# Half of the mixer's convolution and attention output products by seven block products on tiles of 2x2 blocks

## The chip, the cores and the metric

The kernel runs on one core of one Trainium2 chip. The metric is the device time of one execution in microseconds, the median of several runs. A core has five engines with a queue each: TensorE (PE in the profile; its weight loads are listed apart as PEld), VectorE (DVE), ScalarE (ACT), GpSimd (POOL) and SyncE (SP), which here issues the transfers of the weights. An engine takes the instructions of its queue in order, and a semaphore holds an instruction back until what it needs is there.

## The reference, cut to what matters

Two layers of a streaming encoder step work on 640 tokens (512 of a new stream, 8 x 16 of running streams), 1024 wide, in float32. Each layer is a feed-forward half step, a mixer, and a second feed-forward half step. The change is in the mixer, whose last part is:

```
g = jax.nn.sigmoid(g + b_gate)
g_conv, g_attn = jnp.split(g, 2, axis=-1)
y_conv, conv_new = _short_conv(cb, cc, cv, conv_prev, w_conv)      # 512 channels
k_new, v_new, y_attn = ...                                         # attention, 8 heads x 64 = 512 channels
m = g_conv * (y_conv @ w_conv_out) + g_attn * (y_attn @ w_attn_out)
return m @ w_o, conv_new, k_new, v_new
```

`y_conv @ w_conv_out` and `y_attn @ w_attn_out` are products of 640x512 with 512x1024. All the outputs of the step (both token groups, the new keys, values and convolution states) are written.

## The kernel before, in words

**Numbers.** Everything lies transposed: 128 channels on the partitions, the 640 tokens along the free axis. One output tile is 128 channels x 640 tokens. Every operand of a product is split into a high part (a cast to fp32r by ScalarE, which TensorE takes) and a low part (operand minus high part, by VectorE); a product is three matmuls, high x high, high x low and low x high (`multiply`, line 412; the first factor is the weight here, so the order is: weight high with both parts of the operand, then weight low). A matmul takes 320 tokens, half of a tile.

**Weights.** All weights come as one stream of slabs of 128x1024 (eight tiles of 128x128), in the order in which TensorE uses them; the host lays them out in `_stream` by the same list that the device code walks (`mixer_order`, line 114; `stages`, line 136, turns it into kinds of slabs). SyncE loads them into three buffers in turn. A *plain* slab is eight tiles of weights, read one by one by `product`. A *mixed* unit is two slabs in memory, of which VectorE forms sums, so that four slabs of weights come out: for seven block products instead of eight on 2x2 blocks (blocks over two output tiles, two halves of the contraction, two halves of the tokens). `source` (line 293) forms the raw slab, with these sums for a mixed unit:

```
elif arg == 1:
    flush()
    st = sums[n] = spool[0].tile([P, CH // 2], F32, tag="s6", name=f"s6_{n}", bufs=1)
    add(ra[:, h1], ra[:, h1], rb[:, h1])
    add(st, ra[:, h1], rb[:, h2])
    add(rb[:, h1], rb[:, h1], rb[:, h2])
```

and one more sum for the third slab of the unit. `prep` (line 332) casts a slab on ScalarE and notes its low part as pending; `flush` (line 348) issues the pending low parts on VectorE. `slab` (line 355) hands out the next slab and prepares the one two after it; with `hold` set, the low part waits for the next `flush` in the text. `quiet` hands out a slab without preparing one, `ahead` forms the sums of the next slab that isn't prepared.

**The mixer's second part**, `outputs` (line 1463), is what the change rewrites. Before it, attention and the first of the eight pairs of gate tiles have run. It issues its work in an order written out by hand, and TensorE, VectorE and ScalarE keep it (`ORDERED`). Its pieces:
- `gate_pair(m)` (line 1473): two tiles of the gates as seven block products of 12 matmuls, on three banks of PSUM `pa`, `pb`, `pc` (rows `qa`, `qb`, `qc`) out of four that go round. `qa` takes blocks one, three, five and seven: block one is copied out by ScalarE (`c1`, row `capsm`) before block three is added onto it, and so on. VectorE forms `u` and `g` from the blocks, multiplies by the norm's factor `rr`, ScalarE applies the sigmoid (line 1328). Between, VectorE does the low parts (`wlo`, line 350) of the next slabs, and `ahead` stands after block five. A function `then` can be hung in before block six.
- `out(m, y)` (line 1516): one tile of `y @ w` in one of two accumulators `py` that alternate, 4 tiles of contraction x 3 x 2 = 24 matmuls, and the product with the gate on VectorE (line 1524, for the convolution into `mm`; line 1526 for the attention, with a sum onto `mm` after it). A function `then` is called between the matmuls and that product.
- `take` splits the four tiles of `y` into high and low parts (line 235), `give` those of the finished `m`.

The order is: gate pair 2 with `take` of the convolution, outputs 0 to 3, then six times a gate pair (4, 6, 8, 10, 12, 14) with two outputs behind it: 4 to 7 of the convolution and, after a `take` of the attention in pair 8, 8 to 15, which are the attention's outputs 0 to 7. So each pair stands between outputs. After them comes `m @ w_o`, eight products of 48 matmuls (row `po`).

Of the kernel before, what the change touches and what calls it, by code (L numbers as in the profile page):

```python
# [10 lines left out]
F32 = mybir.dt.float32  # L11
# [5 lines left out]
P = 128  # L17
# [38 lines left out]
)  # L56

ROWS = (1, 2)

MARGIN = 2, 4  # L60
LEAN = {"a0": (1, 6), "b0": (1, 5), "a1": (1, 5), "b1": (1, 5)}
# [66 lines left out]


def kinds():  # L130
# [5 lines left out]
def stages():  # L136

    out, done = [], []

    def end(kind):  # L140
        done.append((kind, out[:]))
        out.clear()

    def plain(n):
        out.extend([8] * (n // 8) + [n % 8] * (n % 8 > 0))

    def ffn(name):
        held = 0
        for what, a in ffn_order(name):
            if what == "gu":  # L150
                plain(held)
                held = 0
                out.append("gu")
            elif what == "std":
                held += 2 * KT
            elif what == "cut":
                plain(held)
                held = 0
            elif what == "rows":
                plain(held)  # L160
                held = 0
                out.append("gu")
            elif what == "ends":
                held += KT * len(a)
            else:
                held += sum(len(js) for _, js in a)
        plain(held)

    for l in range(L):
        ffn(f"a{l}")  # L170
        end("ffn")
        held = 0
        for what, _ in mixer_order():
            if what == "mix":
# [12 lines left out]
def two(ps):  # L187
    return ps[:, :, :HT]


def halves(t):
    return t.rearrange("p (a b) -> p a b", a=2)
# [3 lines left out]
def trunk(ctx: ExitStack, tc: tile.TileContext, xin, wst, small, pbias, samplebias, kcache, vcache, gfin,  # L196
# [1114 lines left out]
    def mixer(l, after):  # L1311
        with tc.tile_pool(name=f"yp{l}", bufs=1, reuse_waits="tile") as yp, \
# [84 lines left out]
            with tc.tile_pool(name=f"gp{l}", bufs=1, reuse_waits="tile") as gp, \  # L1397
                 tc.manual_schedule(engines=ORDERED):
                hold[0] = True
                mo = outputs(l, gp, ops.X, st, cs, ycs, yas, sigmoid, gates)  # L1400
        ex = after()
        with tc.manual_schedule(engines=ORDERED):
            hold[0] = True
# [56 lines left out]
        def t5(self, kp):  # L1460
            self.parts(*(z[:, HT:] for z in self.h[2 * kp]), self.a[kp][:, 1])

    def outputs(l, gp, X, st, cs, ycs, yas, sigmoid, gates):


        rr, t1, t2 = st.rr, slice(0, HT), slice(HT, T)
        spare = [gp.tile([P, 2, T], F32, name=f"mm{l}_{i}") for i in range(2)]
        mm = ycs + [spare[i // 2][:, i % 2] for i in range(CT)]
        X11, X21, X22, XN6, XT5, XT7, XT4 = (X[i] for i in ("11", "21", "22", "N6", "T5", "T7", "T4"))
        c1, u2, c5 = cs  # L1470
        every = range(NP)
# [56 lines left out]
            flush()  # L1528

        yc, ya, mo = [], [], []  # L1530

        def take(y, name, srcs):
# [496 lines left out]
def _stream(i):  # L2029
# [9 lines left out]
    for l in range(L):  # L2039
        def ffn(name, gu, down):  # L2040
            g, u = _cols(gu[:, :FF]), _cols(gu[:, FF:])
            d = _cols(down)
            parts, held = [], []
            for what, a in ffn_order(name):
                if what == "gu":
                    if held:
                        parts.append(chunks(held))
                    held = []

                    parts.append(chunks([z[a][o::2] for z in (u, g) for o in range(2)]))  # L2050
# [24 lines left out]
        held = []  # L2075
        for what, m in mixer_order():
            if what == "v":
                out.append(v.reshape(KT // 2, 2, P, AW).transpose(0, 2, 1, 3).reshape(-1, P, CH))
            elif what == "mix":
                out.append(chunks(held))  # L2080
                held = []

                out.append(chunks([rows[name][a][o::2] for name, a in m for o in range(2)]))
            else:
# [73 lines left out]
```

## Time and profile before

| | |
|---|---|
| time, median of 3 runs | 2491.59 us (2491.12 to 2491.73) |
| profiled execution, its own time | 2491.9 us |
| its span | 2490.1 us |
| second part of the mixer, layer 0 | 636 to 778.6 us, 142.6 us |
| granted TensorE clock | 1.00 |

The page gives busy time by engine. A busy TensorE there is the union of overlapping matmuls, so the spacing of their starts is read for the price of one. In a list in order of time, a row is start, duration, engine, line, operation, output and inputs by the program's names, and in brackets the idle time ahead of it with what ended it. In the list by stretches each engine has its busy time in the stretch, with the number of instructions, then the granted clock, the share of the DMA engines and GB/s. Layer 1 repeats the second part from 1918 us on with the same spacings.

### The profile page before, as it was taken

To read this page: it belongs to the slowest core of one execution; us is meant where nothing else is said; L and a number is where in the kernel's file an instruction comes from. 1 tells how busy PE (TensorE), PEld (TensorE's weight loads), DVE (VectorE), ACT (ScalarE), POOL (GpSimd) and SP (SyncE) were. 2 spreads that over 40 slices of the span, in tenths; PEclk is the share of its full clock that TensorE was granted. 3 is DMA by queue.
4 is the path that set the end of the run, shared out by engine and by line. 5 is a ranking of instruction groups with operands and counts; after the bars stand their busy time and mean duration, and the time that the engine had idled before them with its cause. 6 is when DMAs were issued, how large, how long until landed. Compare 5 with 4: busy or idle time off the path is not lost.

```text
span 2490.1 us, 43907 instructions
## 1 busy us (share of the span) xinstructions
PE 2475.0 (99%) x17312; PEld 2422.6 (97%) x17312; DVE 2140.2 (86%) x3532; ACT 1355.9 (54%) x2151; POOL 294.9 (12%) x449
## 2 busy tenths in 40 slices
PE   9999999999999999999999999999999999999998
PEld 8999999889999999999999999998999999999998
DVE  7999998888777899998799999998886769999997
ACT  6555556665444555555665555556644455555555
POOL 0111112211000001111001111121110000111111
PEclk9999999999999999999999999999999999999999
DMA  4443444335223333444334343453342233444444
GB/s 155 126 117 101 123 119 121 114 107 174 77 83 112 94 101 106 112 117 121 98 94 109 110 119 101 115 128 111 128 157 86 77 110 91 108 112 107 111 117 117
DMA packets 109422, 279.22 MB, mean 112 GB/s; under 512 B 12416, under 2 KB 51456, under 8 KB 109216
## 3 DMA queue, kind: packets, MB, share of 16 engines
q1 hardware_dynamic: 68976, 219.44, 26.9%
q0 software_dynamic: 39520, 56.08, 12.0%
q8 instruction: 135, 2.21, 0.4%
q10 hardware_dynamic: 720, 0.91, 0.1%
q14 instruction: 71, 0.58, 0.1%
HBM read 230.56 MB, written 7.94 MB: 96 GB/s over the span
## 4 chain that ended last, share of the span: by engine, by line
PE 93%; DVE 4%; ACT 2%; issue 1%; DMA 0%; ACTq 0%; SPq 0%; DVEq 0%; POOLq 0%
PE pab L440 12%; PE paa L440 11%; PE pcb L440 6%; PE daa L1118 6%; PE pca L440 5%; PE dab L1118 5%; PE py L416 4%; PE po L416 4%; PE qa L440 4%; PE pbb L440 3%; PE dca L1118 3%; PE pba L440 3%; PE dcb L1118 2%; PE ma_cv L440 2%; PE ma_qk L440 2%; PE pv L1605 2%
## 5 line engine op out<-in xcount | busy, mean ns | idle before, releaser
L350 DVE TENSOR_TENSOR wlo<-raw,whi 128x1024 fp32r<-128x1024 f32 (+1 forms) x569 | 580.3, 1022 | 156.1 <-ACT whi L345 152.9
L345 ACT CAST whi<-raw 128x1024 fp32r<-128x1024 f32 (+1 forms) x569 | 505.1, 891 | 381.7 <-PE pbb L440 47.2
L345 ACT CAST whi<-s 128x1024 fp32r<-128x1024 f32 (+1 forms) x158 | 150.3, 952 | 296.0 <-issue 111.3
L440 PE MATMUL pab<-xhib,whi 128*128 128x320 f32 x704 | 217.7, 309 | 0.0
L440 PE MATMUL pab<-xlob,whi 128*128 128x320 f32 x704 | 217.3, 309 | 0.0
L440 PE MATMUL pab<-xhib,wlo 128*128 128x320 f32 x704 | 217.3, 309 | 0.0
L440 PE MATMUL paa<-xloa,whi 128*128 128x320 f32 x640 | 197.6, 309 | 0.6 <-DVE xloa L677 0.6
L440 PE MATMUL paa<-xhia,whi 128*128 128x320 f32 x640 | 198.0, 309 | 0.2 <-DVE ga L287 0.2
L440 PE MATMUL paa<-xhia,wlo 128*128 128x320 f32 x640 | 197.6, 309 | 0.0
L350 DVE TENSOR_TENSOR wlo<-s,whi 128x1024 fp32r<-128x1024 f32 (+1 forms) x158 | 173.5, 1098 | 4.4 <-ACT whi L345 4.4
L1140 POOL DMA_DIRECT2D x<-c_a x80 | 69.9, 1021 | 574.9 <-ACT ahia L1022 205.6
L440 PEld LDWEIGHTS pab<-xhib,whi 128*128 128x128 f32 x704 | 132.1, 188 | 0.9 <-issue 0.9
L440 PEld LDWEIGHTS pab<-xhib,wlo 128*128 128x128 f32 x704 | 132.2, 188 | 0.0
L440 PEld LDWEIGHTS pab<-xlob,whi 128*128 128x128 f32 x704 | 132.2, 188 | 0.0
L1140 POOL DMA_DIRECT2D x<-c_b x72 | 62.7, 1001 | 582.9 <-ACT ahib L1022 205.8
L440 PEld LDWEIGHTS paa<-xhia,whi 128*128 128x128 f32 x640 | 120.1, 188 | 1.3 <-DVE ga L287 0.5
L440 PEld LDWEIGHTS paa<-xloa,whi 128*128 128x128 f32 x640 | 120.1, 188 | 1.1 <-DVE xloa L677 1.1
L440 PEld LDWEIGHTS paa<-xhia,wlo 128*128 128x128 f32 x640 | 120.1, 188 | 0.2
L440 PE MATMUL pcb<-xhib,wlo 128*128 128x320 f32 x352 | 108.9, 309 | 0.0
L440 PE MATMUL pcb<-xhib,whi 128*128 128x320 f32 x352 | 108.7, 309 | 0.0
L440 PE MATMUL pcb<-xlob,whi 128*128 128x320 f32 x352 | 108.7, 309 | 0.0
L287 DVE TENSOR_TENSOR raw<-s,raw 128x512 f32<-128x512 f32 x158 | 107.9, 683 | 0.0
(757 smaller groups left out, 8076.8 us busy)
## 6 DMA issues: line engine op xcount, KB each, us to landing
raw<-in_wst SPq DMA_DIRECT2D x375, 512.0 KB, 3.4
x<-c_a POOLq DMA_DIRECT2D x80, 160.0 KB, 4.4
x<-c_b POOLq DMA_DIRECT2D x72, 160.0 KB, 3.7
lent<-in_wst POOLq DMA_DIRECT2D x34, 256.0 KB, 3.7
kc<-in_kcache SPq DMA_DIRECT2D x32, 256.0 KB, 4.5
vc<-in_vcache SPq DMA_DIRECT2D x16, 512.0 KB, 4.5
x<-u_a POOLq DMA_DIRECT2D x40, 160.0 KB, 3.9
x<-u_b POOLq DMA_DIRECT2D x36, 160.0 KB, 4.0
```

The costliest lines, as they stand in the source:

```text
L287: DVE.tensor_tensor(out=out, in0=a, in1=b, op=op)
L345: ACT.copy(hi[:, d], src[:, c])
L350: DVE.tensor_tensor(out=lo, in0=src, in1=hi.bitcast(F32), op=ALU.subtract)
L416: PE.matmul(ps[:, a, :HT], w, x[a] if isinstance(x, tuple) else x[:, a * HT : (a + 1) * HT], start=first and j == 0 and not seeded, stop=l ...
L440: PE.matmul(ps, a, b, start=start and kp == 0 and j == 0, stop=stop and kp == NP - 1 and j == 2, skip_group_check=True)
L1118: PE.matmul(ps[u], w, y, start=start and i == 0 and j == 0, stop=i == 1 and j == 2, skip_group_check=True)
L1140: POOL.dma_start(x[ms[2 * u + r]][:, cols], z[:, u], accum_op=ALU.add)
L1605: PE.matmul(pv[t], xx[:, t * P : (t + 1) * P], w[:, kk * AW : (kk + 1) * AW], start=c == 0 and kk == 0 and j == 0, stop=c == KT // 2 - 1 a ...
```

## The change

In each branch four of the eight output tiles, 4 to 7 of the convolution and 2 to 5 of the attention (`SEVEN`), are computed together by a new function `rows`: four output tiles as 2x2 blocks, seven block products of 12 matmuls instead of four products of 24. Their weights come as mixed units, in the form of the gate pairs'. The operands of the seven products that are mixtures of tiles of `y` are made by a new function `mixed`, in the memory of `y` itself once its plain parts are taken, with a copy to high parts on ScalarE and a low part on VectorE; it is hung into outputs 0, 1 (and 2) of the branch, the last low part of the attention into gate pair 10. Outputs 0 to 3 now go into the spare tiles, 4 to 7 into the memory of the convolution's `y`. The order becomes: pair 2, outputs 0 to 3, pairs 4 and 6, `rows` for the convolution, pair 8, outputs 8 and 9, pairs 10 and 12, `rows` for the attention, pair 14, outputs 14 and 15.

```diff
     gates = [mix(("g", m), ("g", m + 1)) for m in range(0, 2 * KT, 2)]
-    out += gates[:2] + [("co", m) for m in range(4)]
-    for i, g in enumerate(gates[2:]):
-        name, m = ("co", 4 + 2 * i) if i < 2 else ("ao", 2 * i - 4)
-        out += [g, (name, m), (name, m + 1)]
-    return out + [("o", m) for m in range(KT)]
+    out += gates[:2] + [("co", m) for m in range(4)] + gates[2:4] + [("rows", ("co", SEVEN["co"]))]
+    out += [gates[4], ("ao", 0), ("ao", 1), gates[5], gates[6], ("rows", ("ao", SEVEN["ao"]))]
+    return out + [gates[7], ("ao", 6), ("ao", 7)] + [("o", m) for m in range(KT)]
...
-        mm = ycs + [spare[i // 2][:, i % 2] for i in range(CT)]
+        ycs = [z[:, i] for z in ycp for i in range(2)]
+        mm = [spare[i // 2][:, i % 2] for i in range(CT)] + ycs
+        stage = [halves(st.caps)] + [gp.tile([P, 2, HT], F32, name=f"rs{l}_{i}") for i in range(2)]
...
+        def mixed(z):
+
+            z = z.rearrange("p c (a b) -> p (c a) b", a=2)
+            e1, e2, o1, o2 = (z[:, i] for i in range(4))
+            add(e1, e1, e2, ALU.subtract)
+            add(e2, o2, e2, ALU.subtract)
+            for out, a in ((o2, e1), (o1, o2)):
+                DVE.scalar_tensor_tensor(out=out, in0=a, scalar=-1.0, in1=out, op0=ALU.mult, op1=ALU.subtract)
+            i = len(more) % 2
+            hi, lo = (gp.tile([P, 4, HT], F32R, tag=f"x{i}{p}", name=f"x{p}{l}_{len(more)}") for p in ("hi", "lo"))
+            ACT.copy(hi, z)
+            more.append((hi, lo))
+            return lambda: DVE.tensor_tensor(out=lo, in0=z, in1=hi.bitcast(F32), op=ALU.subtract)
...
+        def rows(name, y):
...
+            A, B = (acc(f"r{i}{n}") for i in "ab")
+            a, b = ([z[:, u, :HT] for u in range(2)] for z in (A, B))
+            c = [att(f"rc{n}_{u}")[:, :HT] for u in range(2)]
+            s1, s2, s5 = stage
...
+            w = quiet()
+            mul(a, w, 0, X11, True)
+            ACT.copy(s1, two(A))
+            prep(used[0] + 1)
+            flush()
+            mul(b, w, 1, X21, True)
+            add(s1, two(B), s1)
+            w = slab(True)[0]
+            flush()
+            mul(a, w, 0, XN6, False)
+            ACT.copy(s2, two(A))
+            gated(0, [s1[:, u] for u in range(2)], t1)
+            mul(c, w, 1, XT5, True)
+            for u in range(2):
+                ACT.copy(s5[:, u], c[u])
+            w = slab(True)[0]
+            mul(a, w, 0, XT7, False)
+            add(s5, two(A), s5)
+            flush()
+            ahead()
+            gated(1, [s5[:, u] for u in range(2)], t2, -1.0)
+            mul(c, w, 1, X22, False)
+            for u in range(2):
+                add(s2[:, u], c[u], s2[:, u])
+            w = slab(True)[0]
+            gated(0, [s2[:, u] for u in range(2)], t2)
+            mul(a, w, 0, XT4, False)
+            flush()
+            gated(1, a, t1, -1.0)
+            total(0)
+            total(1)
+
+        lo = []
         gate_pair(2, lambda: take(yc, "yc", ycs))
-        for m in range(4):
-            out(m, yc)
-        for m in range(4, 2 * KT, 2):
-            gate_pair(m, (lambda: take(ya, "ya", [yas[:, c, :] for c in range(CT)])) if m == KT else None)
-            y = yc if m < KT else ya
-            last = m == 2 * KT - 2
-            out(m, y, (lambda: give(range(3))) if last else None)
-            out(m + 1, y, (lambda: give(range(3, 6))) if last else None)
+        out(0, yc, lambda: lo.append(mixed(ycp[0])))
+        out(1, yc, lambda: (lo[0](), lo.append(mixed(ycp[1]))))
+        out(2, yc, lambda: lo[1]())
+        out(3, yc)
+        gate_pair(4)
+        gate_pair(6)
+        rows("co", yc)
+        gate_pair(8, lambda: take(ya, "ya", [yas[:, c, :] for c in range(CT)]))
+        out(8, ya, lambda: lo.append(mixed(yas[:, 0:2])))
+        out(9, ya, lambda: (lo[2](), lo.append(mixed(yas[:, 2:4]))))
+        gate_pair(10, lambda: lo[3]())
+        gate_pair(12)
+        rows("ao", ya)
+        gate_pair(14)
+        out(14, ya, lambda: give(range(3)))
+        out(15, ya, lambda: give(range(3, 6)))
         give(range(6, KT))
```

In `rows`, `mul` is 12 matmuls into two tiles, `gated` two VectorE products of 128x320 with a half of two gate tiles, and `total` two sums of 128x640 onto `mm`, for the attention only. The host's `_stream` lays the four tiles of a group out as the two slabs of a mixed unit.

More of the change, by code (lines that the diff above doesn't have):

```diff
@@ L58 @@
 ROWS = (1, 2)
+SEVEN = {"co": (4, 5, 6, 7), "ao": (2, 3, 4, 5)}
 MARGIN = 2, 4
@@ L173, in stages @@
         for what, _ in mixer_order():
-            if what == "mix":
+            if what in ("mix", "rows"):
                 plain(held)
@@ L1530, in outputs @@
         yc, ya, mo = [], [], []
+        more = []
         def take(y, name, srcs):
@@ new lines, in kind, with mul, gated, total @@
+        def kind(y, i, k):
+            if k in EXTRA:
+                return tuple(z[:, EXTRA.index(k)] for z in more[i - 2])
+            hi, lo = y[2 * i + (k in (X21, X22))]
+            return tuple(z[:, t2 if k == X22 else t1] for z in (hi, lo))
+        EXTRA = XT5, XT7, XT4, XN6
+        def rows(name, y):
+            n = f"{name}{l}"
+            ms = SEVEN[name]
+            gs = [gates[m + (KT if name == "ao" else 0)] for m in ms]
+            A, B = (acc(f"r{i}{n}") for i in "ab")
+            a, b = ([z[:, u, :HT] for u in range(2)] for z in (A, B))
+            c = [att(f"rc{n}_{u}")[:, :HT] for u in range(2)]
+            s1, s2, s5 = stage
+            def mul(ps, s, half, k, start):
+                for u in range(2):
+                    for i in range(2):
+                        kp = half * NP + 2 * u + i
+                        wh, wl = (z[:, kp * P : (kp + 1) * P] for z in s)
+                        xh, xl = kind(y, i, k)
+                        for j, (w, x_) in enumerate(((wh, xh), (wh, xl), (wl, xh))):
+                            PE.matmul(ps[u], w, x_, start=start and i == 0 and j == 0,
+                                      stop=i == 1 and j == 2, skip_group_check=True)
+            def gated(r, src, t, scale=None):
+                for u in range(2):
+                    g = gs[2 * r + u][:, t]
+                    out = mm[ms[2 * r + u]][:, t] if name == "co" else g
+                    if scale is None:
+                        DVE.tensor_tensor(out=out, in0=src[u], in1=g, op=ALU.mult)
+                    else:
+                        DVE.scalar_tensor_tensor(out=out, in0=src[u], scalar=scale, in1=g,
+                                                 op0=ALU.mult, op1=ALU.mult)
+            def total(r):
+                if name == "ao":
+                    for u in range(2):
+                        add(mm[ms[2 * r + u]], mm[ms[2 * r + u]], gs[2 * r + u])
+            w = quiet()
[11 more added lines that the diff above has]
+            mul(c, w, 1, XT5, True)
+            for u in range(2):
+                ACT.copy(s5[:, u], c[u])
[6 more added lines that the diff above has]
+            mul(c, w, 1, X22, False)
+            for u in range(2):
+                add(s2[:, u], c[u], s2[:, u])
[6 more added lines that the diff above has]
+            total(1)
@@ L2083, in _stream @@
                 out.append(chunks([rows[name][a][o::2] for name, a in m for o in range(2)]))
+            elif what == "rows":
+                out.append(chunks(held))
+                held = []
+                name, ms = m
+                out.append(chunks([rows[name][a][o::2] for r in range(2) for o in range(2)
+                                   for a in ms[2 * r : 2 * r + 2]]))
             else:
```

4 lines of the change are left out of this document (2 added, 2 removed).

## The prediction

> **What bounds the kernel now.** I read the page first, then the busy times of the output stage in eight stretches, then the three queues of that stage in order of time.
>
> ```profile
> span 2490.1 us, 43907 instructions
> PE 2475.0 (99%) x17312; PEld 2422.6 (97%) x17312; DVE 2140.2 (86%) x3532; ACT 1355.9 (54%) x2151; POOL 294.9 (12%) x449
> ```
>
> TensorE is busy 99% of the span; VectorE 86% over all. The diff touches only the second half of each mixer, in layer 0 from 636 to 778.6 us.
>
> ```profile
> 649.00:662.50 13.50, 13.50 (x95) 13.50 (x93) 10.64 (x15) 5.62 (x8) 0.00 (x0) 1.00 0.19 67
> 720.50:739.90 19.40, 19.40 (x135) 19.40 (x134) 16.55 (x24) 7.79 (x12) 0.00 (x0) 1.00 0.25 82
> sum 142.60, PE 142.60 PEld 142.60 DVE 103.23 ACT 66.31 POOL 0.00; mean PE 17.82 PEld 17.82 DVE 12.90 ACT 8.29 POOL 0.00
> ```
>
> There TensorE (first number after the length) has no gap, VectorE is busy 103.2 of 142.6 us and ScalarE 66.3. So a matmul that is saved is time saved, as long as TensorE is still fed. The start times of its matmuls give the price of one:
>
> ```profile
> 662.50 0.31 PE L440 MATMUL qa<-hhim,whi 128*128 128x320 f32 x1
> 664.25 0.31 PE L440 MATMUL qb<-hhim,whi 128*128 128x320 f32 x1
> ...
> 727.55 0.31 PE L440 MATMUL qa<-thi,whi 128*128 128x320 f32 x1
> 727.84 0.31 PE L440 MATMUL qa<-thi,wlo 128*128 128x320 f32 x1
> ```
>
> The durations of 0.31 us overlap; what counts is the spacing. A block product has 12 matmuls: block one of a gate pair starts at 662.50 and block two at 664.25, 1.76 us or 0.1466 us each. A gate pair (7 blocks) is 12.32 us, an output of 24 matmuls 3.52 us, and 12.32 + 2 x 3.52 = 19.36 us is the distance from one gate pair to the next. The rows at 727.55 and 727.84, used in (e), are the first and third matmul of block five of a later pair.
>
> **What is removed.** Four outputs were 4 x 24 = 96 matmuls; seven block products are 84. So 12 x 0.1466 = 1.76 us go per group. Two groups in each of two layers: 7.04 us, if TensorE never waits. That is the whole possible gain, 0.28%.
>
> **What is added.** The operands' work lies on VectorE and ScalarE, whose rows are these (start, duration; the distance to the next start is the price when nothing is waited for):
>
> ```profile
> 671.56 0.49 DVE L287 TENSOR_TENSOR g<-qa,c 128x320 f32<-128x320 f32 x1 [3.47 <-PE qa L440]
> 672.08 0.49 DVE L1493 TENSOR_TENSOR g<-g,rrm 128x320 f32<-128x320 f32 x1
> 672.49 1.22 DVE L350 TENSOR_TENSOR wlo<-raw,whi 128x1024 fp32r<-128x1024 f32 x1
> 673.63 0.48 DVE L287 TENSOR_TENSOR g<-qc,capsm 128x320 f32<-128x320 f32 x1
> 674.15 0.82 DVE L1501 TENSOR_TENSOR g<-g,rrm 128x640 f32<-128x640 f32 x1
> 675.00 0.49 DVE L1507 TENSOR_TENSOR g<-qa,rrm 128x320 f32<-128x320 f32 x1
> ...
> 795.89 0.49 DVE L601 SCALAR_TENSOR_TENSOR xob<-xeb,xob 128x320 f32<-128x320 f32 x1
> 796.41 0.49 DVE L601 SCALAR_TENSOR_TENSOR xob<-xob 128x320 f32<-128x320 f32 x1
> 796.82 0.48 DVE L603 TENSOR_TENSOR xob<-xob,xeb 128x320 f32<-128x320 f32 x1
> ...
> 2035.75 1.15 DVE L677 TENSOR_TENSOR xlob<-xob,xhib 128x960 fp32r<-128x960 f32 x1
> 2036.82 0.82 DVE L287 TENSOR_TENSOR ssumb<-ssumb,sqb 128x640 f32<-128x640 f32 x1
> ```
>
> A 128x320 operation costs 0.41 us, 0.52 where the next one needs its result; a low part of 1024 costs 1.14. The low part of 960 costs 1.07 (2035.75 to 2036.82), of 640 about 0.74, so one of 1280 is taken as 1.40.
> - `mixed`, twice per branch: four operations in place (0.41 + 0.41 + 0.52 + 0.41 = 1.75) and a low part of 1280 (1.40): 6.3 us of VectorE per branch.
> - Weights: two plain slabs (2 x 1.14) become four mixed ones: low parts 1.14 + 2 x 0.605 + 1.14 + 0.605 = 4.1 and four sums of 512, 2.55 (rows below). Together 6.65.
> - `rows` itself: two sums of 640 (1.48), two of 320 and eight gated products of 320 (10 x 0.41): 5.6; for the attention branch four sums of 640 more, 2.95. So 12.2 and 15.2 us, against 5.2 and 8.7 for the four outputs they replace.
>
> VectorE gets (12.2 - 5.2) + 6.3 = 13.3 and (15.2 - 8.7) + 6.3 = 12.8, 26 us a layer: 103 + 26 = 129 of 139 us. On average it still fits. What decides is the order: a queue takes its instructions as written, TensorE has two prepared slabs in hand, and three gate pairs or row groups now follow each other without outputs between. ScalarE's added casts and copies (four of 1280, three of 1024, four of 640, four of 320; about 13 us a layer by the 0.71 for 640 quoted in (c)) fit beside its 66 us and matter at one place below. The weights' transfers stay the same in number and bytes, and POOL gets nothing.
>
> ```profile
> raw<-in_wst SPq DMA_DIRECT2D x375, 512.0 KB, 3.4
> ```
>
> A mixed unit's second transfer goes into the buffer that the unit before it frees with its third slab's low part, and lands 3.4 us later (last number). In the tightest place, gate pair 10, which would be waiting for that low part, its use comes 1.76 (block five) + 0.26 + 0.93 + 1.14 = 4.1 us later (the rows from 671.56): I take it as covered, with 0.7 us to spare; a later landing costs what goes beyond that.
>
> **Six places, stepped through with these prices** (layer 0).
>
> *(a) Outputs 2 and 3 wait for their accumulators.* Two accumulators alternate, and `out` puts `mixed` in front of the product that empties one.
>
> ```profile
> 651.85 1.21 DVE L350 TENSOR_TENSOR wlo<-raw,whi 128x1024 fp32r<-128x1024 f32 x1
> 653.15 0.82 DVE L1524 TENSOR_TENSOR yc<-py,g 128x640 f32<-128x640 f32 x1
> 655.53 1.23 DVE L350 TENSOR_TENSOR wlo<-raw,whi 128x1024 fp32r<-128x1024 f32 x1 [1.55 <-ACT whi L345]
> 656.67 0.82 DVE L1524 TENSOR_TENSOR yc<-py,g 128x640 f32<-128x640 f32 x1
> ```
>
> Now: low part until 652.99, mixed until 654.74, product of output 0 until 655.56 (starts at 653.15 today), low part of the gate's weights until 656.69, low part of the mixture until 658.09, second mixture until 659.84, product of output 1 until 660.66. Output 2 is due at 662.50 - 2 x 3.52 = 655.46 and output 3, then, at 659.1: 0.15 + 1.6 = 1.75 us lost.
>
> *(b) Gate pair straight after gate pair.* From the rows above: block five of the pair at 662.50 ends at 671.30, and the last product out of its bank `qa` ends at 675.49, 4.19 later. With a mixed unit next, `ahead` puts three sums (1.94, rows below) in between: 6.13. With four banks and three per pair, the next pair's second block takes just that bank, 3 x 1.76 = 5.28 after: 0.85 us lost (pair 4 to 6). From pair 10 to 12 the last mixture's low part (1.40) stands there too: 2.25.
>
> *(c) Gate pair to rows.* `rows` copies its first block out on ScalarE, behind the pair's two sigmoids.
>
> ```profile
> 675.00 1.56 ACT L1328 ACTIVATE g<-g,sm 128x640 f32<-128x640 f32 x2 [0.86 <-DVE g L1501]
> ...
> L1132 ACT ACTIVATE c_a<-daa x20: 687/707/707, 96.6 to 1637.0; 128x640 f32<-128x640 f32 x20
> ```
>
> They end at 676.56, 5.26 after block five, 7.20 with the sums; the copy (0.71, row of the same shape) ends at 7.91. Block three, which adds onto that bank, is due at 7.04: 0.87 lost, in both branches.
>
> *(d) Rows (convolution) to gate pair 8.* Counted from the end of rows' block five: VectorE starts at 0.23, sum 0.74, low part 1.14, three sums 1.94, two gated 0.81, two sums 0.91, two gated 0.81, low parts until 7.87. The next unit's third block needs them at its third matmul (the first two of a triple use the high part), 7.33: 0.54 lost. Then, from 7.79, gated 0.81, weight sum 0.68, cast 1.18, low part 1.23 (the last three as in the rows under (e), 724.49 to 727.58), until 11.69, for block five's third matmul at 11.39: 0.3 more. Together 0.84.
>
> *(e) Outputs 8, 9 to gate pair 10.* Here today's trace has no slack:
>
> ```profile
> 718.16 0.69 DVE L287 TENSOR_TENSOR raw<-raw,raw 128x512 f32<-128x512 f32 x1
> 718.89 0.69 DVE L287 TENSOR_TENSOR s<-raw,raw 128x512 f32<-128x512 f32 x1
> 719.50 0.69 DVE L287 TENSOR_TENSOR raw<-raw 128x512 f32<-128x512 f32 x1
> 720.10 0.82 DVE L1526 TENSOR_TENSOR g<-py,g 128x640 f32<-128x640 f32 x1
> ...
> 722.90 0.82 DVE L1526 TENSOR_TENSOR g<-py,g 128x640 f32<-128x640 f32 x1
> 723.75 0.83 DVE L287 TENSOR_TENSOR yc<-yc,g 128x640 f32<-128x640 f32 x1
> 724.49 0.68 DVE L287 TENSOR_TENSOR raw<-s,raw 128x512 f32<-128x512 f32 x1
> 726.35 1.23 DVE L350 TENSOR_TENSOR wlo<-raw,whi 128x1024 fp32r<-128x1024 f32 x1 [1.17 <-ACT whi L345]
> ```
>
> VectorE runs without a gap from the sums at 718.16 to the weight sum at 724.49; ScalarE casts, and the low part ends at 727.58. The matmul that needs it starts at 727.84: 0.26 us to spare. Two mixtures and one low part (2 x 1.75 + 1.40 = 4.90) are put in ahead: 4.64 lost.
>
> *(f) Rows (attention) to gate pair 14.* As (d), with `total`'s four sums (2.95) ahead of the weight sum: 0.84 + 2.95 = 3.79.
>
> **Sum.** First half 1.75 + 0.85 + 0.87 + 0.84 = 4.3; second 4.64 + 2.25 + 0.87 + 3.79 = 11.55; 15.85 us of waits a layer against 3.52 gained: +12.3, and twice that, +24.6 us. The profiled execution takes 2491.9 us (span 2490.1 and 1.8 around it; 0.3 over the median of the runs): 2516.5, against the median 2516.2. I predict 2516 us. Bounds: the prices of in-place and 1280-element operations are by the nearest rows; half a microsecond either way at each of 16 waits is 8 us. If (e) and (f) were only half (a queue that runs less strictly in order than I step it), 8 less again.
>
> **Rivals.**
> - *The lead covers it: faster.* If the prepared slabs and VectorE's 10 us of spare time a layer absorbed every step, 7.04 go: 2484.9. For it: the average. Against: the 0.26 us in (e), and (a), which is a wait on an accumulator that no slab helps. It ends below today only if less than 3.52 of the 15.85 us remain. In between, waits near 3.5 a layer give no change (0.2%, 5 us, is about what a measurement tells apart here).
> - *TensorE slows down after long waits.* At the start of the program it does:
>
> ```profile
> 5.27 0.64 PE L416 MATMUL poa<-xhia,whi 128*128 128x320 f32 x1 [5.27 <-ACT whi L733]
> ...
> 12.99 0.47 PE L416 MATMUL poa<-x2hia,whi 128*128 128x320 f32 x1
> 13.26 0.42 PE L416 MATMUL poa<-xloa,whi 128*128 128x320 f32 x1
> ...
> 13.66 0.31 PE L416 MATMUL poa<-xhia,wlo 128*128 128x320 f32 x1
> 13.81 0.31 PE L416 MATMUL poa<-x2hia,wlo 128*128 128x320 f32 x1
> ```
>
> From 5.27 to 13.3 matmuls start 0.27 apart, then 0.15. If waits (e) and (f), 4 and 3 us, bring that back, each costs up to 8.1 x (1 - 0.147/0.267) = 3.6 us: two (e alone) give 2523.5, four 2530.7. Against: no wait of that length inside the span shows it, since there is none. [...]
>
> **How the numbers follow.** My forecast 0.74, with 2506 to 2526 as its own range; the slow spells 0.12; the covered case 0.09; no change 0.05. Most of what would make me wrong makes the loss smaller, so the range goes from 2500 (both bounds below) to 2531 (four slow spells). Faster 0.09, same 0.05, slower 0.86.
>
> **What would show it.** TensorE's busy time in the stage falls by 3.5 us a layer while its idle time appears: behind the product that empties `py` before output 3, behind `g` at the second block of pairs 6 and 12, behind the first copy in `rows`, and behind `wlo` in pairs 8, 10 and 14, the largest in 10 and 14. VectorE's busy time rises by some 50 us in all. If those waits are missing, or VectorE idles in pairs 10 and 14, the prediction is wrong; spacings of 0.27 us after the waits would speak for the clock.

## The result, and the profile after

The changed kernel takes 2528.6 us (2528.0 to 2529.8), the kernel before 2491.6 us (2491.1 to 2491.7): 37.0 us more, a ratio of 1.015 (95% interval 1.0137 to 1.0162). The profiled execution took 2528.5 us. The head of its page:

```profile
span 2526.7 us, 43949 instructions
PE 2481.1 (98%) x17264; PEld 2423.2 (96%) x17264; DVE 2192.1 (87%) x3632; ACT 1379.6 (55%) x2187; POOL 295.6 (12%) x449
...
PE 84%; DVE 10%; ACT 3%; issue 2%; DMA 1%; SPq 0%; ACTq 0%; DVEq 0%; POOLq 0%
```

Before, the same line of the chain (the work that ended last, by engine) read:

```profile
PE 93%; DVE 4%; ACT 2%; issue 1%; DMA 0%; ACTq 0%; SPq 0%; DVEq 0%; POOLq 0%
```

Instructions: TensorE has 48 fewer matmuls, 12 for each of four groups; VectorE has 100 more instructions and 51.9 us more work, near the 50 foretold. The chain that ends last now runs 10% of the span over VectorE and 3% over ScalarE: the time that TensorE waits for them. The second part of the mixer in layer 0, in the view by stretches (length, then busy time of TensorE, its weight loads, VectorE, ScalarE, POOL, then the granted clock):

```profile
635.40:796.30 160.90, 145.61 (x951) 142.89 (x950) 128.50 (x196) 77.65 (x115) 0.00 (x0) 0.97 0.23 76
```

By the starts of its first matmul and of the first one after it, the stage takes 160.8 us, 18.4 us longer than before (142.4 us), and layer 1 loses as much. VectorE is busy 128.5 us of it, where 129 was forecast, and not full: what costs is the order. The view of waits, TensorE's only (line, what ended the wait; total, times, longest), over both layers:

```profile
PE qa L440 <- ACT capsm L1481: 16.4, 6, 5.8
PE qa L440 <- ACT capsm L1489: 7.8, 4, 3.4
...
PE py L416 <- DVE mm L1526: 3.3, 4, 1.5
PE raao L1582 <- ACT capsm L1602: 1.5, 2, 0.8
PE raco L1582 <- ACT capsm L1602: 1.5, 2, 0.8
```

These five groups, 30.5 us, of which 27.2 end with a copy on ScalarE, have no counterpart in the same view of the kernel before, where no wait of the stage is above 0.2 us. `capsm` at L1481 is ScalarE's copy of a pair's block one (`c1`), at L1489 of block three (`u2`), at L1602 the first copy in `rows`. The longest wait, ahead of block three of gate pair 10, in TensorE's queue in order of time:

```profile
732.61 0.64 PE L440 MATMUL qa<-thi,whi 128*128 128x320 f32 x1 [5.81 <-ACT capsm L1481]
733.04 0.47 PE L440 MATMUL qa<-tlo,whi 128*128 128x320 f32 x1
733.31 0.47 PE L440 MATMUL qa<-thi,wlo 128*128 128x320 f32 x1
...
737.57 0.43 PE L440 MATMUL qc<-hhim,whi 128*128 128x320 f32 x1
737.84 0.31 PE L440 MATMUL qc<-hlom,whi 128*128 128x320 f32 x1
737.99 0.31 PE L440 MATMUL qc<-hhim,wlo 128*128 128x320 f32 x1
```

Two things are to be seen. The wait ends with a copy on ScalarE, not with a low part on VectorE. And the matmuls after it start 0.27 us apart until 737.84, then 0.15. The granted clock in the same place, by stretches:

```profile
734.00:738.00 4.00, 4.00 (x18) 4.00 (x17) 2.22 (x3) 1.21 (x3) 0.00 (x0) 0.52 0.37 111
738.00:742.00 4.00, 4.00 (x30) 4.00 (x29) 1.37 (x3) 1.37 (x2) 0.00 (x0) 1.00 0.42 152
```

It is 0.52 of full speed for these 4 us and 1.00 after. Why the copy is late stands in ScalarE's queue:

```profile
724.79 1.27 ACT L1553 CAST xhi<-ya 128x1280 fp32r<-128x1280 f32 x1 [1.36 <-DVE ya L1550]
730.97 1.26 ACT L1553 CAST xhi<-ya 128x1280 fp32r<-128x1280 f32 x1 [4.91 <-DVE ya L1550]
732.13 0.42 ACT L1481 COPY capsm<-qa 128x320 f32<-128x320 f32 x1
733.22 1.57 ACT L345 CAST whi<-raw 128x1024 fp32r<-128x1024 f32 x2 [0.67 <-DVE raw L287]
```

The copy of 0.42 us at 732.13 is queued behind the cast of the second mixture (730.97), and that cast was held 4.91 us for VectorE's mixture (L1550), whose last two operations VectorE reached at 729.91, behind all that outputs 8 and 9 had put ahead of them:

```profile
728.87 1.01 DVE L287 TENSOR_TENSOR ya<-ya 128x320 f32<-128x320 f32 x2
729.91 1.02 DVE L1550 SCALAR_TENSOR_TENSOR ya<-ya 128x320 f32<-128x320 f32 x2
```

Before the change no instruction of this kind stood in ScalarE's queue ahead of that copy.

Put together for layer 0, forecast in brackets. A wait is taken here, and below, as the distance from one start to the next less 0.147 us, which is 0.16 more than the idle time in a row's bracket: (a) 2.00 us (1.75); (b) 0.66 (0.85) and 2.05 (2.25); (c) 0.91 (0.87) and 0.92 (0.87); (d) 0.64 (0.84); (e) 5.97 (4.64); (f) 3.59 (3.79). Together 16.7 us (15.85). Layer 1 repeats each to 0.02 us. Behind the long waits come stretches of matmuls at 0.27 us, five in all, of 18, 10, 11, 14 and 14 matmuls, which cost 2.1, 1.2, 1.25, 1.6 and 1.6 us, 7.7 in all. So of the 37.0 us: waits 33.5, less the 7.0 of the 48 matmuls, and 7.7 of slow matmuls; of the 2.8 that are left, 1.6 are the first one or two matmuls after each of the other waits (the spans of the two profiled executions, in which all this is read, differ by 36.6 and not 37.0), and the rest I have not put down to anything.

### The profile page after: what moved, and what is told of

It reads as the page before. It is cut to its first block, busy times and chain, and to the rows that moved or that the text cites. A ratio compares the mean times of both kernels' runs of the same rounds, so it can differ in the third digit from the quotient of the medians.

```text
span 2526.7 us, 43949 instructions
## 1 busy us (share of the span) xinstructions
PE 2481.1 (98%) x17264; PEld 2423.2 (96%) x17264; DVE 2192.1 (87%) x3632; ACT 1379.6 (55%) x2187; POOL 295.6 (12%) x449
## 4 chain that ended last, share of the span: by engine, by line
PE 84%; DVE 10%; ACT 3%; issue 2%; DMA 1%; SPq 0%; ACTq 0%; DVEq 0%; POOLq 0%
PE pab L440 12%; PE paa L440 11%; PE pcb L440 6%; PE daa L1118 6%; PE pca L440 5%; PE dab L1118 5%; PE po L416 4%; PE pbb L440 3%; PE dca L1118 3%; PE pba L440 3%; PE dcb L1118 2%; DVE wlo L350 2%; PE ma_cv L440 2%; PE ma_qk L440 2%; PE pv L1706 2%; PE qa L440 2%
## 5 line engine op out<-in xcount | busy, mean ns | idle before, releaser
L287 DVE TENSOR_TENSOR raw<-s,raw 128x512 f32<-128x512 f32 x162 | 110.6, 683 | 0.0
```

The lines of the kernel that those rows point to most:

```text
L287: DVE.tensor_tensor(out=out, in0=a, in1=b, op=op)
```

## The experiments

My theory was that the loss is the order in three queues, as forecast but with ScalarE's added, and that the clock comes on top. Against it stood that the amount of work, or `rows` itself, is what costs. The kernel before took 2491.1 to 2491.5 us in these comparisons. Where a helper was added, line numbers are shifted.

### Is it the wait or the clock?

`warm` fills two of the waits with matmuls that nothing uses:

```diff
+        def idle(s, n):
+            z = acc(f"idle{l}_{n}")
+            for i in range(n):
+                PE.matmul(z[:, 0, :HT], s[0][:, :P], X11(0)[0], start=i == 0, stop=i == n - 1)
...
+            if m == 10:
+                idle(s0, 32)
             block(pa, s1, 0, XN6, every, False, True)
...
+            if m == 14:
+                idle(s1, 18)
             block(pa, s2, 0, XT7, every, False, True)
```

> Edit: 32 extra matmuls of 320 columns into an unused accumulator in gate pair 10 ahead of block three, 18 in gate pair 14 ahead of block five, so that TensorE works inside the two long waits (6.0 and 3.6 us) instead of idling; nothing reads them. Theory (the waits are set by the other queues, and the doubled spacing after them is TensorE's clock falling after idling): the waits keep their places, the 29 or so matmuls per layer at 0.27 us go back to 0.147, 3.5 us a layer, so about 2521.5 us, and the granted clock is 1.00. Rival (the doubled spacing has another cause, or the extra matmuls come on top): 2528.6 or more, the spacing still 0.27 behind the waits.

Measured: 2522.9 us (2522.1 to 2524.1), ratio 1.0126 (1.0111 to 1.0142), 5.65 us less than the changed kernel although 100 matmuls were added. TensorE's queue at the same place:

```profile
726.66 4.86 PE L1478 MATMUL idle<-hhim,whi 128*128 128x320 f32 x32
732.63 0.42 PE L440 MATMUL qa<-thi,whi 128*128 128x320 f32 x1 [1.11 <-ACT capsm L1486]
732.89 0.32 PE L440 MATMUL qa<-tlo,whi 128*128 128x320 f32 x1
733.04 0.32 PE L440 MATMUL qa<-thi,wlo 128*128 128x320 f32 x1
...
733.20 0.31 PE L440 MATMUL qa<-thi,whi 128*128 128x320 f32 x1
```

Block three starts at 732.63 as before: the 32 matmuls took 4.69 us of the wait, 1.28 us of it were left, 5.97 together. So the length of the wait is set by the other queues and not by TensorE. But now the matmuls behind it start 0.15 apart from its second on, at a granted clock of 1.00 (733 to 737 us; 0.52 above). In pair 14 it is 2.65 + 0.94 = 3.59. Of the five slow stretches one is left (1.5 us, layer 1, after the 2.05 us wait in pair 12, which was not filled). The four stretches that are gone had cost 6.1 us, and the time fell by 5.65. So the clock's part is shown: about 6 us of the loss are the clock after long waits.

### Which branch?

`co_only` and `ao_only` leave one branch as before the change:

```diff
 co_only
-        gate_pair(10, lambda: lo[3]())
+        gate_pair(10)
+        out(10, ya)
+        out(11, ya)
         gate_pair(12)
-        rows("ao", ya)
+        out(12, ya)
+        out(13, ya)
...
 ao_only
         gate_pair(4)
+        out(4, yc)
+        out(5, yc)
         gate_pair(6)
-        rows("co", yc)
+        out(6, yc)
+        out(7, yc)
```

(shortened: the other hooks of `mixed` and the order of the weights go with them.)

> Edit: the seven products for the convolution only; the attention as before the change. Theory (each place has its own wait): per layer the waits ahead of outputs 2 and 3, of pair 6, of rows and of pair 8 stay, 4.2 and some 0.6 of restarts against 1.76 gained: +3 us a layer, 2497.5 us, no wait over 2 us, clock 1.00. Rival (the added VectorE work as a whole, 13.3 of 26 us a layer, sets the loss): half of the change's 37 us, 2510 us.

Measured: 2498.0 us (2497.4 to 2498.8), ratio 1.0026 (1.0016 to 1.0036). Waits of 2.01 (two together, 0.38 and 1.63), 0.66, 0.91 and 0.64 us in layer 0, no slow stretch, clock 1.000.

> Edit: the seven products for the attention only; the convolution as before the change. Theory: per layer the waits at pair 10 (6.0), pair 12 (2.05), rows (0.9) and pair 14 (3.6) stay, with some 4.5 of slow matmuls and restarts, against 1.76: +15.3 us a layer, 2522 us. Rival (VectorE's work as a whole): 2510 us.

Measured: 2522.3 us (2521.3 to 2523.3), ratio 1.0124 (1.0108 to 1.0139). Waits of 6.03, 2.06, 0.91 and 3.58 us, and five slow stretches. The two losses, 6.5 and 30.8 us, add up to the whole (37.3 against 37.0). `rows` is in both, with the same seven products; what differs is what is queued around it. That speaks against `rows` itself as the cause.

### Step (e): the mixture in front of pair 10

`mix_late` takes the second mixture out of output 9:

```diff
-        out(9, ya, lambda: (lo[2](), lo.append(mixed(yas[:, 2:4]))))
-        gate_pair(10, lambda: lo[3]())
-        gate_pair(12)
+        out(9, ya, lambda: lo[2]())
+        gate_pair(10, lambda: lo.append(mixed(yas[:, 2:4])))
+        gate_pair(12, lambda: lo[3]())
```

> Edit: the attention's second mixture moves from output 9 into gate pair 10 (behind block five's products), its low part into gate pair 12. Theory (in pair 10 block three waits because ScalarE's copy of block one stands behind the second mixture's cast, which waits for VectorE): block three of pair 10 waits under 1 us, block five about 2.5 us for the weights' low part and the copy behind its cast, no slow clock there; pair 12 waits 0.3 more, rows 1.4 more: 3.4 us a layer less, 2522 us. Rival (only the amount of VectorE work ahead of the weights' low part counts): the wait in pair 10 falls by the 1.75 of the mixture alone and comes back as 1.75 later, 2528 less the clock's 4.4: 2524 us, with block three still waiting.

Measured: 2529.9 us (2529.4 to 2530.1), ratio 1.0154 (1.0139 to 1.0169): nothing gained. ScalarE's queue and then TensorE's:

```profile
724.92 1.27 ACT L1553 CAST xhi<-ya 128x1280 fp32r<-128x1280 f32 x1 [1.36 <-DVE ya L1550]
726.08 0.42 ACT L1481 COPY capsm<-qa 128x320 f32<-128x320 f32 x1
731.37 1.56 ACT L345 CAST whi<-raw 128x1024 fp32r<-128x1024 f32 x2 [4.87 <-DVE raw L287]
732.84 0.42 ACT L1489 COPY capsm<-qa 128x320 f32<-128x320 f32 x1
```

```profile
733.31 0.42 PE L440 MATMUL qa<-thi,whi 128*128 128x320 f32 x1 [2.67 <-ACT capsm L1489]
...
761.01 0.42 PE L1582 MATMUL raao<-xhi,whi 128*128 128x320 f32 x1 [2.15 <-ACT capsm L1602]
```

The copy of block one now comes at 726.08 and block three no longer waits: the cause of the 5.97 us is shown. In its place block five waits 2.82 us, for a copy (732.84) behind a cast that waits for the weight sum, L287. That is the place that step (e) had named, and the size fits: 4.64 less the mixture of 1.75 is 2.89. So the forecast wait was there too, hidden behind a longer one. The moved work then delays pair 12 (2.40 us in layer 0 for 2.05; 3.51 in layer 1, which I have not explained) and `rows` (2.31 for 0.92). In layer 0 these waits are nearly the ones I expected (2.5, 0.3 more and 1.4 more). My miss is the clock: I expected it to stay up in pair 10, but slow stretches come after the waits of 2.82, 2.31 and 3.51 as well, seven in all where the changed kernel has five, and they take back what the waits give.

### Step (f): `total` in front of the weight sum

`no_total` leaves out the four sums of the attention's last groups onto `mm` (`if name == "ao"` becomes a condition that never holds), so four output tiles lack the attention's part of `m`.

> Edit: the four sums that end the attention's rows are left out (the attention's part of output tiles 2 to 5 is not added, so those outputs are incomplete). Theory: with 2.95 us less in VectorE's queue ahead of the sum for pair 14's third slab, the wait at block five of pair 14 falls from 3.6 to 0.64 us as in pair 8, and no slow clock follows: 4.4 us a layer, 2520 us; VectorE's instructions around it keep their lengths. Rival (pair 14 waits for something else): 2528.6 us less nothing, the wait still 3 us or more.

Measured: 2520.2 us (2519.8 to 2520.6), ratio 1.0117 (1.0103 to 1.013).

```profile
779.30 0.41 PE L440 MATMUL qa<-thi,whi 128*128 128x320 f32 x1 [0.49 <-ACT capsm L1489]
```

The wait in pair 14 is down from 3.59 to 0.65 us, as in pair 8, and no slow stretch follows it. 2.94 us of waits a layer are the 2.95 of the four sums: the share of `total` in step (f) as foretold.

### Could GpSimd, idle here, take the work?

`pool_total` gives it only `total`; `pool_both` also the mixtures and their low parts; `best` has the same as `pool_both`, with some of the order changed besides.

```diff
-                        add(mm[ms[2 * r + u]], mm[ms[2 * r + u]], gs[2 * r + u])
+                        z = mm[ms[2 * r + u]]
+                        POOL.tensor_tensor(out=z, in0=z, in1=gs[2 * r + u], op=ALU.add)
```

> Edit: the four sums of 640 that end the attention's rows (total) run on GpSimd instead of VectorE. Theory: they stand in VectorE's queue ahead of the sum for pair 14's third slab; without them the wait at block five of pair 14 falls from 3.6 to 0.64 us as in pair 8, no slow clock follows it (1.2 to 1.6 us), 4.4 us a layer: 2520 us. Rival (something else than total delays pair 14): the wait stays at 3.6, 2528.6 us. Unknown: whether VectorE's instructions beside GpSimd's get longer.

> Edit: total and also the four operations and the low part of each mixture run on GpSimd (with the sign made by a fifth operation), both casts of a branch in pair 4 or pair 10. Theory: the waits ahead of outputs 2 and 3 and the long one in pair 10 go, pair 12's falls to pair 6's 0.66; left are 2 x (0.66 + 0.91 + 0.64) = 4.4 us and some 0.8 of restarts a layer against 3.52: +1.7 us a layer, 2495 us, clock 1.00. Rival (the seven products cost by themselves, or GpSimd's work slows VectorE's or comes too late): over 2500 us.

> Edit: as before with GpSimd, and the order of the queues is changed: in pairs 4, 6, 10 and 12 the product that empties bank qa and its sigmoid come ahead of the other tile's, whose product and sigmoid run in the next unit behind the cast of its third slab; the gated products of rows run in the next pair behind that low part. Theory: no wait in the stage is left over 0.3 us, so the 7.04 us of saved matmuls show: 2485 us (2484 to 2488). Rival: VectorE's remaining load, or GpSimd beside it, leaves waits of 3.5 us a layer or more: 2491 us or slower.

Measured: 2530.2 us (2529.6 to 2530.7), ratio 1.0156 (1.0139 to 1.0173); 2539.8 us (2534.8 to 2540.3), 1.0191 (1.0175 to 1.0206); 2526.5 us (2525.4 to 2527.0), 1.0141 (1.0126 to 1.0156). All three missed, by 10 to 45 us. The profile of `pool_both` is of the fastest of its four executions. VectorE's queue in `pool_total`, where the weights' low parts of 512 took 0.68 us each before:

```profile
774.55 2.04 DVE L350 TENSOR_TENSOR wlo<-s,whi 128x512 fp32r<-128x512 f32 x1
776.52 2.05 DVE L350 TENSOR_TENSOR wlo<-raw,whi 128x512 fp32r<-128x512 f32 x1
...
779.29 1.93 DVE L287 TENSOR_TENSOR raw<-s,raw 128x512 f32<-128x512 f32 x1
```

and GpSimd's:

```profile
774.41 3.61 POOL L1599 TENSOR_TENSOR mm<-mm,g 128x640 f32<-128x640 f32 x2 [163.35 <-DVE g L1590]
779.11 3.50 POOL L1599 TENSOR_TENSOR yc<-yc,g 128x640 f32<-128x640 f32 x2 [1.09 <-DVE g L1592]
```

While GpSimd adds (774.41 to 778.02 and 779.11 to 782.61), the low parts take 2.04 and 2.05 us and the weight sum 1.93, three times as long. VectorE loses 4.0 us on these three to be rid of the 2.95 us of `total`, and in layer 0 pair 14 waits 1.38 and 3.06 us in place of 3.59. `best` shows it at its largest, VectorE's queue and then GpSimd's:

```profile
656.61 1.48 DVE L350 TENSOR_TENSOR wlo<-raw,whi 128x1024 fp32r<-128x1024 f32 x1 [1.45 <-ACT whi L345]
658.01 0.81 DVE L1542 TENSOR_TENSOR mm<-py,g 128x640 f32<-128x640 f32 x1
...
672.52 3.98 DVE L350 TENSOR_TENSOR wlo<-raw,whi 128x1024 fp32r<-128x1024 f32 x1
676.53 3.33 DVE L287 TENSOR_TENSOR raw<-raw,raw 128x512 f32<-128x512 f32 x1
679.89 0.69 DVE L287 TENSOR_TENSOR s<-raw,raw 128x512 f32<-128x512 f32 x1
```

```profile
656.13 4.02 POOL L1565 TENSOR_TENSOR yc<-yc 128x320 f32<-128x320 f32 x3
...
672.37 6.94 POOL L1578 TENSOR_TENSOR xlo<-yc,xhi 128x1280 fp32r<-128x1280 f32 x2 [10.80 <-ACT xhi L1577]
```

1.22 and 0.69 us have become 3.98 and 3.33 while GpSimd makes two low parts (672.37 to 679.31); right after, 0.69 again. `pool_both` has the same at this place (3.97 and 3.33). The product at 658.01 (`mm<-py,g`) takes its usual 0.81 beside GpSimd; and the low part at 656.61 shows that the stretch is not always so large (1.48 for 1.22). So what VectorE handed over came back as longer instructions of its own.

### Is it the amount or the order?

`order_both` has the work of the changed kernel on the same engines (3632 instructions on VectorE, 2190.7 us against 2192.1) and moves it in the queues: mixtures behind the products that empty `py`; the last factor and sigmoids of pairs 4, 6, 10 and 12 to the start of the next unit; the last products of `rows` and half of `total` likewise; the attention's mixtures into pairs 10 and 12 and their low parts to the start of `rows`.

```diff
+            due(rest)
             flush()
+            due(last)
...
+            def whole():
+                DVE.tensor_tensor(out=u, in0=u, in1=rr, op=ALU.mult)
+                sigmoid(u, m)
...
             flush()
+            if m in (4, 6, 10, 12):
+                rest.append(whole)
...
-            gated(0, [s2[:, u] for u in range(2)], t2)
             mul(a, w, 0, XT4, False)
             flush()
-            gated(1, a, t1, -1.0)
-            total(0)
-            total(1)
+            last.append(lambda: (gated(1, a, t1, -1.0), gated(0, [s2[:, u] for u in range(2)], t2), total(0)))
+            sums.append(lambda: total(1))
...
+        out(0, yc, post=lambda: (mixed(ycp[0]), cast.pop()()))
...
+        gate_pair(10, lambda: due(cast), lambda: mixed(yas[:, 0:2]))
+        gate_pair(12, lambda: due(cast), lambda: mixed(yas[:, 2:4]))
+        rows("ao", ya, low)
+        gate_pair(14, lambda: due(sums))
```

> Edit: all the work of the change stays on VectorE and ScalarE, only its order is changed: conv mixtures behind the products that empty the accumulators; in pairs 4, 6, 10 and 12 the product that empties bank qa and its sigmoid first, the other tile's product and sigmoid in the next unit; part of rows' gated products in the next pair behind its third slab's low part; the attention's mixtures in pairs 10 and 12 behind block two's sum and the fourth slab's low part, their casts behind block five, their low parts at the start of rows; total in pair 14. Theory (the loss is the order, not the amount of work): conv side no wait over 0.4 us, attention side about 0.6 in pair 12, 1.3 in rows, 0.7 in pair 14, no slow clock: 2489 us (2485 to 2493). Rival (VectorE's amount of work, 129 of 139 us, is what TensorE can't be fed beside): the waits only move, as they did when one mixture was moved, and the time stays over 2505 us.

Measured: 2497.4 us (2497.1 to 2499.1), ratio 1.0026 (1.0016 to 1.0036): 31 of the 37 us are back, with nothing taken from VectorE. So for these 31 us it is the order, and not the amount of work. But it is 8 us more than I expected and outside the 2485 to 2493 that I gave: the last 6 us, and the 7 us of the saved matmuls, did not come back. TensorE's queue:

```profile
748.62 0.41 PE L1602 MATMUL raao<-xlo,whi 128*128 128x320 f32 x1 [0.74 <-DVE xlo L1575]
...
750.02 0.41 PE L1602 MATMUL raao<-xlo,whi 128*128 128x320 f32 x1 [0.69 <-DVE xlo L1575]
...
750.86 0.47 PE L1602 MATMUL raao<-xhi,whi 128*128 128x320 f32 x1
751.13 0.47 PE L1602 MATMUL raao<-xlo,whi 128*128 128x320 f32 x1
...
781.66 0.53 PE L416 MATMUL po<-m_0hi,whi 128*128 128x320 f32 x2 [1.63 <-ACT m_5hi L234]
788.10 0.55 PE L416 MATMUL po<-m_6lo,whi 128*128 128x320 f32 x2 [0.63 <-DVE m_6lo L235]
```

The attention's low parts, now late themselves, hold `rows` twice (0.94 and 0.85 us by the starts), 14 slow matmuls follow in layer 0 (none in layer 1), and the first product of `m @ w_o` waits 1.80 and 0.79 us (by the starts) for `m`'s parts, behind the moved sums. Either VectorE has no place left in this stage at which the attention's mixtures delay nobody, or I did not find it: for the attention's half, the amount of work is not ruled out.

`order_co` is the convolution's half of that, with the attention as before the change.

> Edit: the seven products for the convolution only, in the changed order of the run beside it; the attention as before the change. Theory: no wait over 0.4 us is left on the convolution's side, the 3.52 us of saved matmuls show: 2488 us. Rival: waits of 1.8 us a layer or more are left, 2491 us or slower (2498.0 in the change's own order).

Measured, in 11 runs: 2488.6 us (2488.4 to 2489.0) against 2491.2 (2490.9 to 2491.7), ratio 0.999 (0.9981 to 0.9998): 2.65 us faster than the kernel before. Its page:

```profile
span 2486.6 us, 43930 instructions
PE 2471.3 (99%) x17288; PEld 2418.7 (97%) x17288; DVE 2165.6 (87%) x3582; ACT 1366.9 (55%) x2169; POOL 295.6 (12%) x449
```

24 matmuls fewer are 3.52 us; no wait in the stage is over 0.36 us and no slow stretch is left. So three quarters of the promised gain of this half are there once no queue is late. The other quarter is one wait a layer, 0.30 us ahead of block three of pair 4 (668.90) and 0.2 in the first matmuls behind it.

## Why the prediction was right, and where it was wrong

The direction was right, and so was the main cause, the order in the queues. The time lies in the range, but above the 2506 to 2526 us that the forecast had for itself: the allowance for four slow spells covers it. The likeliest value was 12.6 us too low.

- *What is removed*: 48 matmuls, and `order_co` gives 2.65 of the 3.52 us of its half where no wait is over 0.36 us.
- *What is added*: VectorE's work came out as stepped (128.5 us in the stage for 129, the low part of 1280 at 1.40 us from 727.47 to 728.87). "On average it still fits. What decides is the order" is what `order_both` shows for most of the loss.
- *(a) and (c)*: 2.00 us for 1.75, and 0.91 and 0.92 for 0.87, where and why the forecast said (in (a), 655.56 less 655.46 is 0.10 and not 0.15).
- *(b)*: 0.66 and 2.05 us for 0.85 and 2.25, but the place and the cause were wrong, so that the nearness is luck. VectorE's product out of pair 4's `qa` came when it was stepped, ending 6.14 us after block five for 6.13. Yet block two of pair 6, which was to wait for it, starts before it:

```profile
678.10 0.31 PE L440 MATMUL qb<-hhim,whi 128*128 128x320 f32 x1
678.49 0.48 DVE L1509 TENSOR_TENSOR g<-qa,rrm 128x320 f32<-128x320 f32 x1
...
680.06 0.40 ACT L1481 COPY capsm<-qa 128x320 f32<-128x320 f32 x1
...
680.52 0.41 PE L440 MATMUL qa<-thi,whi 128*128 128x320 f32 x1 [0.50 <-ACT capsm L1481]
```

So it does not take that bank. What waits is block three, for the copy of block one, which stands in ScalarE's queue behind the sigmoids: the case that (c) had stepped for `rows` alone. Its steps with a copy of 0.42 us give 7.20 + 0.42 - 7.04 = 0.58 here and, with the low part of 1.40, 1.98 for pair 12.
- *(d)*: the forecast had two waits for low parts, 0.54 us at block three and 0.30 at block five, 0.84 together. Block three waits for nothing worth naming (its third matmul starts at 706.58, before the second of the two low parts ends at 707.12), and block five waits 0.64, for a copy on ScalarE behind the casts of the same slabs. In (f) it is the same copy.
- *(f)*: 3.59 us for 3.79, and `no_total` confirms the share of `total`.
- *(e)*: this step failed most, in place and size. I let ScalarE's added casts "fit beside its 66 us and matter at one place below", the copy in (c). There was a second place: the cast of the second mixture stands ahead of the copy of pair 10's block one and waits for VectorE, and so the wait came two blocks earlier and at 5.97 us for 4.64. The steps of VectorE alone were right for block five, as `mix_late` shows (2.82 for 2.89). Worth 1.3 us a layer, 2.7 in all. With (b), (d) and (f) it is the same omission: ScalarE's short copies were stepped in (c) alone.
- *The rival "TensorE slows down after long waits"*, held at 0.12, came true on top of the forecast: 7.7 us. The reason against it, that no wait in the span showed it, was no reason, since the span had no such waits. Its price of up to 3.6 us a stretch, taken from the start of the program, was too high: 1.2 to 2.1 measured. Its count of four was too low by one, since a wait of 2.04 us sufficed once. This term is most of the miss; the waits together add 1.8 ((e) 2.7 more, the others 0.9 less), and the 2.8 us left over above nearly make up the rest. The spacing of 0.27 us was named as the sign of this rival, and it came.
- *The other signs*: the waits ahead of output 3 and in `rows` came as named; those of the pairs ended with copies and not with `g` or `wlo`. TensorE's busy time in the stage did not fall by 3.5 us but rose (145.6 for 142.4), since slow matmuls count as busy (4.00 of the 4.00 us at a clock of 0.52).
- *"The lead covers it"* fell with the first row of waits.
- The second transfer, covered by 0.7 us by my count, held nothing back: no wait of TensorE in the stage ends with a transfer.

## What to carry to other kernels

When work is put into a queue that is kept in order, step every queue it touches: a cast that waits for another engine delays the short copy behind it, and here that made a wait of 5.97 us out of the 4.64 that VectorE's steps alone gave. Spare time on an engine (10 us of 139 here) says little on whether added work fits; which instruction stands ahead of the one that TensorE needs next does, and reordering alone gave back 31 of 37 us. And price a long wait of TensorE with the slow matmuls after it, 1.2 to 2.1 us a stretch here.

## What the runs showed of the hardware

*TensorE's clock after waits.* In the eight traces of changed kernels in which GpSimd has no added work, every wait from 2.8 us on is followed by 10 to 19 matmuls 0.27 us apart (1.2 to 2.3 us lost). After the waits of 2.04 to 2.06 us, which stand at the same place of both layers, it comes in layer 1 (13 or 14 matmuls) and never in layer 0; after 2.31 us twice, after 2.40 us not. No single wait of up to 1.80 us brings it, but two of 0.94 and 0.85 us, 1.4 us apart, once did. With GpSimd at work, 3.06 us in layer 0 of `pool_total` and 2.79 in layer 1 of `best` did not bring it, and the same waits in the other layer did. So no length alone decides.

A pattern can be read from the ends of the slow stretches. In each of the seven traces with more than one, they lie whole multiples of 3.413 us apart, to 0.25 us, a spacing fitted to these ends (`mix_late`: from 738.30 to 765.59, 1987.38 and 2018.32 it is 8, 366 and 375 times). Each trace has its own offset; in the two with one stretch, its end gives it. Laid over the waits as a grid, this sorts the waits of these traces: where a window of the grid began at full clock and TensorE idled 1.91 us or more of it (the least in `mix_late`, 731.4 to 734.8), the matmuls in the next window were slow, and with up to 1.75 us (the most in `order_both`, 778.2 to 781.6) they were not (of three windows between, 1.78, 1.80 and 1.84 us, the one with 1.80 brought it). The wait of 2.04 us in layer 1 of the changed kernel lies in one window (1997.3 to 2000.7), and the slow matmuls begin at its end, at 2000.75, 1 us after the wait is over; in layer 0 a boundary at 748.0 divides it into 0.65 and 1.40 us. The 3.06 us of `pool_total` are divided into 1.50 and 1.57. Why such a grid fits, no run here shows. With the wait of 5.97 us filled by 32 unused matmuls up to its last 1.28 us (`warm`), the clock behind it stayed at 1.00.

*VectorE beside GpSimd.* I had not expected that instructions of VectorE took three to five times as long beside GpSimd's (0.68 to 2.04 us in `pool_total`, 0.69 to 3.33 in `best`), nor that this cost VectorE more than it was relieved of (4.0 us for 2.95 in `pool_total`). Others beside GpSimd took 1.48 us for 1.22, or their usual 0.81; what tells them apart, no run here shows.
